# Sixteen projection blocks as quarter-sum products in a stage of their own, on one Trainium2 core

## The chip, the core and the metric

The kernel runs on one core of one Trainium2 chip. The metric is the device time of one execution in microseconds (us), the median of several runs. The core has five engines that run their own instruction streams: TensorE (PE) multiplies matrices and transposes, VectorE (DVE) and ScalarE (ACT) do elementwise work and bring results out of PSUM, GpSimd (POOL) does some elementwise work, and SyncE (SP) issues the DMA transfers. "PEld" in a profile is PE's loading of the stationary operand, which overlaps its matmuls.

## What is computed

One block of a hybrid encoder on 1024 tokens of width 1024, all in float32, with 16 learned meta tokens ahead of them:

```python
h = concat(meta_tokens, x)                       # 1040 tokens
u = rmsnorm(h, norm_mix)
a, q, k, v, r, lr, ga, gb = split(u @ w_in)      # widths 512, 256, 256, 512, 512, 16, 1024, 1024
p = (multiscale_pool(a) per group @ w_pool_mix) * pool_scale     # trailing means over 2, 4, 8, 16 tokens
y_a = p @ w_pool_out
log_a = log_sigmoid(lr @ w_gate_up + b_gate) / 16
o = gla_chunked(q / 8, k, v, log_a)              # chunks of 64 tokens, 4 heads, a state carried from chunk to chunk
o = rmsnorm(o, gla_norm) * silu(r)
y_b = o @ w_gla_out
h = h + (sigmoid(ga) * y_a + sigmoid(gb) * y_b) @ w_out
h = h + square(relu(rmsnorm(h, norm_ffn) @ w_ff1)) @ w_ff2
out = rmsnorm(h, norm_final)[16:]
```

## The kernel before

Every large product is made of three matmuls per 128 x 128 x 512 piece: each operand is split into a hi part (an fp32r copy, made by ACT) and a lo part (the rest, a subtraction on DVE), and `mm3` (L234) issues hi by hi, hi by lo and lo by hi into one PSUM bank. Activations are kept transposed: `TH` and `TL` hold the hi and lo parts of the normed input, 8 slices of 128 channels by 512 tokens, for each half of the sequence. A projection block is 128 columns of `w_in`. `project` (L245) runs it for each half of the tokens: 8 slices by 3 matmuls, so 48 matmuls of 512 columns for a block. Its weights come through the ring `W1` (class `Ring`, L57): two slots of 1024 columns, each loaded by SP into a raw buffer, copied to hi by ACT (L75) and subtracted to lo by DVE (L76; in the start stage by POOL). `drive` (L272) tops the ring up before each step.

The stages, in order:

1. `start` (L359). For each of eight tiles of 128 tokens: load, norm (`layer_norm`, L207, with `inv_sqrt`, L185), eight transposes on PE, split out of PSUM (`transposed`, L218, and L183), and the v projection of two heads for that tile (`v_tile`, L320), one tile behind. The meta tokens and the low-rank gate inputs (`lr_turn`, L344) follow.
2. Pooling (steps of L427 to L519). Four blocks of `a` (`a_block`), the trailing means and the mixing product of each (`mix_block`, L443), eight pooling gate blocks (`ga_block`, L479) and four products with `w_pool_out` (`ya_block`, L487), which multiply by the gate and store to DRAM (`ma_dram`). Gate blocks and pooling are interleaved by hand in the list at L512.
3. GLA (`gla`, L810). A chain of small matmuls, scans and state steps: `inside` (L703) makes the scores of a unit (two heads, one half of the tokens) by a level-wise decay, `across` (L735) carries the state and calls `finish` (L786). Both are generators that yield written waits in us: `inside` 4.5, 2.0 and six times LEVEL = 1.6, `across` 3.0, 2.4, and twice 1.0, 0.6, 0.6, 0.6, 4.0. There are four units. `inside` of a unit and `across` of the unit before go round by round; in each round `pour` (L813) puts filling work on PE, as much as the largest wait times PACE = 1.2, by the costs that the filling steps yield (0.64 for three matmuls). The filling work is the list `fill` (L632): k and q, the second half of v, four output gate blocks (`r_block`, L570), eight blocks of the other gate (`gb_block`, L580), and the first half of the product with `w_gla_out` (`yb_block`, L597). The order on PE is the order in which the program writes it; the other engines' order is laid out by the framework's planner, in which work written earlier goes first among what is ready.
4. Merge and output product, then the squared-ReLU MLP. The MLP's first product (`ff1`, L1080) already uses quarters: the channels and the tokens are cut in half, and for each pair of output blocks seven products of 12 matmuls (P1 to P7) of sums and differences of quarters stand for eight. The weight operands are made three products ahead (`ff1_weights`, L1012), the partial results are added up by DVE with the running sums `u2` and `u3`, and four results come out per pair (A11, A22, A12, A21).

A sigmoid (L468) is an ACT chain of Abs, Exp and Ln, one DVE operation (L474), and a last Exp.

Of the kernel before, what the change touches and what calls it, by code (L numbers as in the profile page):

```python
# [31 lines left out]
PACE, LEVEL = 1.2, 1.6  # L32
# [71 lines left out]
def kernel(  # L104
# [24 lines left out]
    banks(sc=2, mm=3, ms=3)  # L129
# [5 lines left out]
    ma_dram = dp.tile([8, 2, P, HALF], F32, name="ma_dram")  # L135
    gb_dram = dp.tile([8, 2, P, HALF], F32, name="gb_dram")
    r_dram = dp.tile([HEADS, 2, P, HALF], F32, name="r_dram")
# [103 lines left out]

    MAIN = [(0, META, HALF), (1, 0, HALF)]
# [29 lines left out]
    def drive(steps):  # L272

        for ring, aps, fn in steps:
            if fn is not start:
                for r in rings:
                    r.top_up()
# [80 lines left out]

    def start():  # L359
# [7 lines left out]
        mf = left.push("mf", [P, 6, CH], F32)  # L367
        S["vw"] = [right.push("vw0", [P, 2, KT, VP], F32R)]
# [4 lines left out]
        W1.eng = pool  # L373
        for t in range(8):
# [4 lines left out]
            if t == 3:  # L379
                W1.top_up()  # L380
            u = us[:, t % 3]
            layer_norm(xs[:, t % 4], u)
            transposed(u, t // 4, OFF[t // 4] + (t % 4) * P, ("ms", "sc"))
            if t == 0:
                nc.sync.dma_start(S["lrraw"], w_in[:, C_LR : C_LR + 16].rearrange("(k p) c -> p k c", p=P))
                load_vw(0)
                load(1)
                load(2)
                v_tile(0, 0)
            if t == 6:  # L390
                layer_norm(xm, um)
            if t > 1:
                v_tile(0, t - 1)
        transposed(um, 0, 0)
# [5 lines left out]
        W1.eng = dve  # L400
# [3 lines left out]
        nc.sync.dma_start(wgu, w_gate_up)  # L404

    one = []
    step(one, start)


    def pool_open():  # L410
# [11 lines left out]
        buffer("t1", 2)  # L422
        buffer("g", 6)
        buffer("o", 2)
        raw.lend(left.push("raw2", [P, D], F32))

# [16 lines left out]
    def mix_block(g):  # L443
        def fn():
# [9 lines left out]
            wb = (S["mw"][:, 0, g], S["mw"][:, 1, g])  # L454
            for c in halves():
                act.activation(S["ph"][:, 0, c], pp[:, c], ACT.Copy)
                dve.tensor_tensor(S["ph"][:, 1, c], pp[:, c], f32(S["ph"][:, 0, c]), ALU.subtract)
            for tag, c in zip(("ms", "sc"), halves()):
# [20 lines left out]
    def ga_block(d):  # L479
        def evac(b, half, at, n):  # L480
            t = sigmoid(b)
            g = gates[d, half] = nxt("g")
            act.activation(g, t, ACT.Exp)

        return lambda wb: project(wb, MAIN, evac)

    def ya_block(j):  # L487
        def fn(wb):
            hi, lo = (t.rearrange("p (k c) -> p k c", k=4) for t in wb)
            pm = S["pm"]  # L490
            for e in range(2):
                d, w = 2 * j + e, slice(e * P, (e + 1) * P)
                for h, c in enumerate(halves()):
                    b = bank("mm")
                    mm3(b, 4, lambda i: (hi[:, i, w], lo[:, i, w]), lambda i: (pm[:, 0, i, c], pm[:, 1, i, c]))
                    if e and h:
                        yield "free"
                    o = nxt("o")
                    dve.tensor_tensor(o, b, gates.pop((d, h)), ALU.mult)
                    nc.sync.dma_start(ma_dram[d, h], o)  # L500
                    yield 12 * 512 / 2400
# [6 lines left out]
    a_ = lambda g: step(one, a_block(g), W1, [w_cols(C_A + g * P)])  # L508
    m_ = lambda g: step(one, mix_block(g))
    g_ = lambda d: step(one, ga_block(d), W1, [w_cols(C_GA + d * P)])  # L510
# [7 lines left out]
    for f, i in ((g_, 6), (g_, 7), (y_, 3)):  # L518
        f(i)  # L519


    def gla_open():
# [4 lines left out]
        S["q"] = [left.push(f"q{h}", [P, 2, HALF], F32) for h in range(2)]  # L527
        S["v"].append(left.push("v1", [P, 2 * NC, P], F32))
# [25 lines left out]
    def q_block(p):  # L554
        def evac(b, half, at, n):
            act.activation(S["q"][half][:, p, :], b, ACT.Copy, scale=CH ** -0.5)

        return lambda wb: project(wb, MAIN, evac)

# [9 lines left out]

    def r_block(h):  # L570
        def evac(b, half, at, n):
            t = sigmoid(b)
            o = nxt("o")
            act.activation(t, t, ACT.Exp)
            dve.scalar_tensor_tensor(o, b, gnorm[:, h : h + 1], t, ALU.mult, ALU.mult)
            nc.sync.dma_start(r_dram[h, half], o)

        return lambda wb: project(wb, MAIN, evac)

# [52 lines left out]
    for p in range(2):  # L632
        step(fill, k_block(p), W1, [w_cols(C_K + p * P)])
        told(("k", p))
        step(fill, q_block(p), W1, [w_cols(C_Q + p * P)])
        told(("q", p))
        if p == 0:
            step(fill, v_second)
            step(fill, yg_open)
            told("v")  # L640
    for h in range(4):
        step(fill, r_block(h), W1, [w_cols(C_R + h * P)])
        told(("r", h))
    for d in range(8):
# [26 lines left out]
    def meta_state(p):  # L671
# [12 lines left out]
        yield 1.0  # L684
        b = bank("ms")
# [17 lines left out]
    def inside(p, half):  # L703
# [7 lines left out]
        while ("q", p) not in done:  # L711
            yield 1.0
# [22 lines left out]
    def across(p, half):  # L735
# [29 lines left out]
        ends = []  # L765
# [20 lines left out]
    def finish(p, half, g, o):  # L786
        while ("r", 2 * p + 1) not in done:
# [22 lines left out]
    def gla():  # L810
        filler = drive(fill)

        def pour(us):  # L813
            while us > 0:
# [3 lines left out]
                us -= cost  # L818

        while ("k", 0) not in done:  # L820
            pour(1e-3)
        units = [(0, 0), (1, 0), (0, 1), (1, 1)]
        old, side = [], [meta_state(0)]
        for n, u in enumerate(units + [None]):
# [9 lines left out]
            if n == 0:  # L834
                while ("k", 1) not in done:
                    pour(1e-3)
# [37 lines left out]
    def wo1_open():  # L874
# [4 lines left out]
        raw.lend(right.push("rawx0", [P, D], F32))  # L879
# [25 lines left out]

    def quad(a):
# [405 lines left out]
```

## Time and profile before

| | |
|---|---|
| median of 3 runs | 1293.3 us (1293.14 to 1293.83) |
| the profiled execution's own time | 1293.83 us |
| its span in the profile | 1292.0 us |
| busy: PE, DVE, ACT, POOL | 1258.3, 816.0, 600.6, 81.4 us |
| start stage, until the first pooling matmul | 0 to 60.4 us |
| pooling stage | 60.4 to 255.9 us |
| GLA stage with all its filling work | 255.9 to about 552.8 us |
| merge, output product, MLP | to the end |

The span runs from the first to the last instruction in the trace. The stage ends were read from the timeline on PE: the first matmul of a pooling block, the first log-decay matmul of GLA (L653), and the end of the filling work. A "window" view gives for a stretch of time the busy time of each engine with the count of instructions in brackets. A group of instructions shows its line, its engine, output and inputs, shapes, a count, the busy time in all and the mean in ns, and then the time that the engine stood idle just before them with what ended most of it.

### The profile page before, as it was taken

What the parts mean: (1) busy time and instruction counts of PE and PEld (TensorE: products, weight loads), DVE (VectorE), ACT (ScalarE), POOL (GpSimd) and SP (SyncE); (2) the same over time, 40 slices, a digit from 0 to 9 for tenths busy, and PEclk for the clock granted to TensorE, in tenths of its full rate; (3) what the DMA queues carried; (4) which work ended last, traced back from release to release, by engine and by line L of the source; (5) the groups of instructions that cost most, each with busy time, mean ns of one, the idle gap of its engine ahead of it and who ended that gap; (6) DMA issues with size and microseconds to landing.
All of it is one profiled execution on the core that took longest, in us unless ns stands there. A gap on an engine that the chain in (4) does not pass through costs nothing.

```text
span 1292.0 us, 17890 instructions
## 1 busy us (share of the span) xinstructions
PE 1258.3 (97%) x6703; PEld 1042.4 (81%) x6703; DVE 816.0 (63%) x1367; ACT 600.6 (46%) x1089; POOL 81.4 (6%) x62
## 2 busy tenths in 40 slices
PE   5999999999999999999999999999999999999997
PEld 5888888888788888878878888888887788888776
DVE  6636222263758675763788667677665777887686
ACT  6334334333456645431565455445453444444544
POOL 1000001020203120430000000000000000000000
PEclk9899999999999999999999999999999999999999
DMA  7211223210132323882225444444459873333522
GB/s 233 49 33 49 82 77 104 65 33 18 34 99 75 98 75 113 268 303 65 82 82 187 140 161 147 149 153 152 157 194 360 281 248 113 93 97 90 163 92 88
DMA packets 139191, 164.91 MB, mean 128 GB/s; under 512 B 10432, under 2 KB 84944, under 8 KB 139104
## 3 DMA queue, kind: packets, MB, share of 16 engines
q1 hardware_dynamic: 139104, 163.76, 39.2%
q8 instruction: 53, 0.87, 0.3%
q14 instruction: 34, 0.28, 0.1%
HBM read 115.50 MB, written 48.23 MB: 127 GB/s over the span
## 4 chain that ended last, share of the span: by engine, by line
PE 88%; DVE 5%; DMA 4%; ACT 1%; issue 1%; SPq 0%; DVEq 0%; ACTq 0%
PE b_mm L238 14%; PE b_mm L240 13%; PE b_mm L239 13%; PE b_o L239 7%; PE b_o L240 7%; PE b_o L238 7%; PE b_y L240 3%; PE b_y L238 3%; PE b_y L239 3%; PE b_sc L700 2%; PE b_z L239 2%; PE b_z L240 2%; PE b_z L238 2%; PE b_sc L239 2%; PE b_sc L240 2%; PE b_sc L238 2%
## 5 line engine op out<-in xcount | busy, mean ns | idle before, releaser
L238 PE MATMUL b_mm<-th,w1h 128*128 128x512 f32 (+1 forms) x496 | 189.2, 381 | 0.0
L239 PE MATMUL b_mm<-tl,w1h 128*128 128x512 f32 (+1 forms) x496 | 184.5, 372 | 0.0
L240 PE MATMUL b_mm<-th,w1l 128*128 128x512 f32 (+1 forms) x496 | 184.1, 371 | 0.0
L238 PEld LDWEIGHTS b_mm<-th,w1h 128*128 128x128 f32 x496 | 93.2, 188 | 19.8 <-issue 3.2
L240 PEld LDWEIGHTS b_mm<-th,w1l 128*128 128x128 f32 x496 | 93.3, 188 | 16.9
L239 PEld LDWEIGHTS b_mm<-tl,w1h 128*128 128x128 f32 x496 | 93.3, 188 | 14.6
L76 DVE TENSOR_TENSOR w1l<-raw,w1h 128x1024 fp32r<-128x1024 f32 x38 | 47.9, 1260 | 87.1 <-ACT w1h L75 86.6
L75 ACT ACTIVATE w1h<-raw 128x1024 fp32r<-128x1024 f32 x40 | 42.3, 1057 | 89.2 <-PE b_mm L239 88.1
L238 PE MATMUL b_o<-w1h 128*128 128x512 f32 x192 | 75.2, 392 | 2.7 <-DVE h L1135 1.7
L239 PE MATMUL b_o<-w1l,w1h 128*128 128x512 f32 x192 | 75.2, 391 | 1.3 <-DVE w1l L989 1.3
L240 PE MATMUL b_o<-w1h,w1l 128*128 128x512 f32 x192 | 74.9, 390 | 0.1
L988 ACT ACTIVATE w1h<-raw 128x512 fp32r<-128x512 f32 x88 | 54.6, 623 | 43.4 <-PE b_sc L239 14.1
L989 DVE TENSOR_TENSOR w1l<-raw,w1h 128x512 fp32r<-128x512 f32 x88 | 60.2, 684 | 11.5 <-ACT w1h L988 11.5
L474 DVE SCALAR_TENSOR_TENSOR t<-b_mm,t 128x512 f32<-128x512 f32 x40 | 27.5, 688 | 53.4 <-ACT t L473 53.3
L1183 DVE TENSOR_TENSOR bt<-w,w 128x512 f32<-128x512 f32 x80 | 54.7, 684 | 1.1 <-DMA w<-in_w_ff_dram 1.1
L988 ACT ACTIVATE w1h<-bt 128x512 fp32r<-128x512 f32 x45 | 28.4, 630 | 57.4 <-issue 33.6
L239 PE MATMUL b_o<-fxl,fxh 128*128 128x512 f32 x128 | 50.3, 393 | 0.6 <-DVE small L199 0.6
L238 PE MATMUL b_sc<-th,w1h 128*128 128x512 f32 x128 | 50.1, 391 | 0.7 <-ACT u2p L1107 0.7
L238 PE MATMUL b_mm<-wo,th 128*128 128x512 f32 x128 | 50.7, 396 | 0.0
L239 PE MATMUL b_z<-tl,w1h 128*128 128x512 f32 x128 | 49.9, 390 | 0.4 <-DVE tl L931 0.4
L239 PE MATMUL b_mm<-wo,th 128*128 128x512 f32 x128 | 50.2, 392 | 0.0
L240 PE MATMUL b_mm<-wo,tl 128*128 128x512 f32 x128 | 50.2, 392 | 0.0
(299 smaller groups left out, 3168.9 us busy)
## 6 DMA issues: line engine op xcount, KB each, us to landing
hf_dram<-h SPq DMA_DIRECT2D x112, 256.0 KB, 2.1
raw<-hf_dram SPq DMA_DIRECT2D x112, 256.0 KB, 2.7
raw<-in_w_in_dram SPq DMA_DIRECT2D x32, 512.0 KB, 4.2
w<-in_w_ff_dram SPq DMA_DIRECT2D x64, 256.0 KB, 4.8
rawx<-in_w_ff_dram SPq DMA_DIRECT2D x16, 512.0 KB, 4.1
raw<-in_w_ff_dram SPq DMA_DIRECT2D x16, 512.0 KB, 4.0
xs<-in_x_dram SPq DMA_DIRECT2D x8, 512.0 KB, 5.8
ma_dram<-o SPq DMA_DIRECT2D x16, 256.0 KB, 2.0
```

Of the source, the lines that this page charges most:

```text
L75: self.nc.scalar.activation(hi, raw, ACT.Copy)
L76: self.eng.tensor_tensor(lo, raw, hi.bitcast(F32), ALU.subtract)
L238: pe.matmul(ps, ah, bh, start=first and i == 0, stop=False, skip_group_check=more)
L239: pe.matmul(ps, ah, bl, start=False, stop=False, skip_group_check=more)
L240: pe.matmul(ps, al, bh, start=False, stop=last and i == n - 1, skip_group_check=more)
L474: dve.scalar_tensor_tensor(t, b, 0.0, t, ALU.min, ALU.subtract)
L700: pe.matmul(b[r, c], kk[r, s], qq[r, s], start=True, stop=True, tile_position=(e * CH, e * CH))
L988: act.activation(hi, a, ACT.Copy)
L989: dve.tensor_tensor(lo, a, f32(hi), ALU.subtract)
L1183: dve.tensor_tensor(bt, w, S["w2"][q[3:]][:, i], ALU.add if q[2] == "+" else ALU.subtract)
```

## The change

The scheme of the MLP's first product is taken out into a class, `Quarters`, and used a second time. The eight ga blocks, two q blocks, four r blocks and the first two gb blocks, in that order, form eight pairs, and each pair is made by seven products of 12 matmuls. They are made in a new stage, `gate_stage`, between the start stage and pooling.

- In `start`, `turned` replaces `transposed`: it also builds the four quarter sums of the activations (`ut`), by two more ACT copies for each of the first four tiles, and by one ACT copy and four DVE subtractions for each of the last four. W1 isn't loaded in the start stage any more, so POOL's splits are gone from there. Four products (P1 and P2 of the first two pairs) are issued on PE among the last four tiles.
- `gate_stage` splits the four sums into hi and lo, then runs the other 52 products. Results go through the sigmoid and out to DRAM: ga to `ga_dram` (new), q to `q_dram` (new), r and gb where they went before.
- Pooling has no gate blocks left. Its order is turned round (group 3 first), the means (`mean_block`) and the mixing product (`mix_block`) are separate steps, the first `ya_block` takes the last mixing product into its middle, and gates are loaded from `ga_dram` four ahead.
- In GLA, q is loaded from `q_dram`; `fill` holds k, v, six gb blocks and the product with `w_gla_out`. PACE is 0.91, and `pour` carries over what it poured too much (`owed`). Waits for q and r are replaced by waits for v.
- The PSUM banks of the start stage are two `mm` and four `ms` instead of three and three, of the new stage two `sc`, four `y` and two `z`.

```diff
-PACE, LEVEL = 1.2, 1.6
+PACE, LEVEL = 0.91, 1.6
...
-    banks(sc=2, mm=3, ms=3)
+    banks(sc=2, mm=2, ms=4)
...
+    class Quarters:
...
+        def run(self):
+
+            xb, zb, late = {}, {}, []
+            for p, i, (ah, al) in self.todo():
+                bh, bl = self.x[p]
...
+                mm3(b, 4, lambda k: (ah[:, k], al[:, k]), lambda k: (bh[:, k], bl[:, k]), first=not more, more=more)
+                u2 = S["u2p"][:, i % 2]
+                if p == "P1":
+                    act.activation(u2, b, ACT.Copy)
+                elif p == "P2":
+                    late.append(i)
+                yield
+                while self.room and late:
+                    n = late.pop(0)
+                    self.result(n, A11, xb.pop(n), None)
+                if p == "P6":
+                    dve.tensor_tensor(u2, b, u2, ALU.add)
+                elif p == "P7":
+                    u3 = S["u3p"][:, i % 2]
+                    dve.tensor_tensor(u3, b, u2, ALU.add)
+                    self.result(i, A22, zb[i], u3)
...
+    def turned(u, t):
...
+            if half == 0:
+                act.activation(r[j], b, ACT.Copy)
+            elif j == 0:
+                act.activation(r[2], b, ACT.Copy)
+                dve.tensor_tensor(r[0], b, r[0], ALU.subtract)
+            else:
+                dve.tensor_tensor(r[3], b, r[0], ALU.subtract)
+                dve.tensor_tensor(r[2], b, r[2], ALU.subtract)
+                dve.tensor_tensor(r[1], r[1], r[3], ALU.subtract)
...
-                W1.top_up()
...
+            if t > 3:
+                next(run)
...
+    def gate_result(i, w, b, u):
+        (kind, n, _), half = BLOCKS[2 * i + (w in (A12, A22))], int(w in (A21, A22))
+        if u is not None:
+            c = nxt("c")
+            dve.tensor_tensor(c, b, u, ALU.add)
+            b = c
+        o = nxt("o")
...
+        t = sigmoid(b)
+        if kind == "r":
+            act.activation(t, t, ACT.Exp)
+            dve.scalar_tensor_tensor(o, b, gnorm[:, n : n + 1], t, ALU.mult, ALU.mult)
+            nc.sync.dma_start(r_dram[n, half], o)
+        else:
+            act.activation(o, t, ACT.Exp)
+            nc.sync.dma_start((ga_dram if kind == "ga" else gb_dram)[n, half], o)
+
+    def gate_stage():
...
+        for p, j in (("P5", 0), ("P6", 3), ("P7", 2), ("P4", 1)):
...
+            q.x[p] = h, l = [left.push(f"ut{j}{k}", [P, 4, HALF], F32R) for k in "hl"]
+            for k in range(0, 4, 2):
+                a = S["ut"][j][:, k : k + 2]
+                act.activation(h[:, k : k + 2], a, ACT.Copy)
+                dve.tensor_tensor(l[:, k : k + 2], a, f32(h[:, k : k + 2]), ALU.subtract)
...
+        for _ in S["gate_run"]:
+            pass
...
     for f, i in (
-        (a_, 0), (a_, 1), (m_, 0), (a_, 2), (m_, 1), (a_, 3), (m_, 2), (g_, 0), (m_, 3), (g_, 1),
-        (y_, 0), (g_, 2), (g_, 3), (y_, 1), (g_, 4), (g_, 5), (y_, 2),
+        (a_, 3), (p_, 3), (a_, 2), (m_, 3), (p_, 2), (a_, 1), (m_, 2), (p_, 1), (a_, 0), (m_, 1), (p_, 0),
+        (y_, 0), (y_, 1), (y_, 2),
     ):
...
-    for d in range(8):
+    step(fill, v_second)
+    step(fill, yg_open)
+    told("v")
+    for d in range(2, 8):
         step(fill, gb_block(d), W1, [w_cols(C_GB + d * P)])
...
+        owed = [0.0]
+
         def pour(us):
-            while us > 0:
+            owed[0] += us
+            while owed[0] > 0:
                 cost = next(filler, None)
                 if cost is None:
                     return
-                us -= cost
+                owed[0] -= cost
```

More of the change, by code (lines that the diff above doesn't have):

```diff
@@ L425, in pool_open @@
         raw.lend(left.push("raw2", [P, D], F32))
+        for _ in range(4):
+            gate_load()
     step(one, pool_open)
@@ L477, with gate_load @@
     gates = {}
[L479 to L485, printed above, removed]
+    def gate_load():
+        n = len(gates)
+        if n < 16:
+            g = gates[n // 2, n % 2] = nxt("g")
+            nc.sync.dma_start(g, ga_dram[n // 2, n % 2])
     def ya_block(j):
@@ L684, in meta_state @@
         yield 1.0
+        while p and "v" not in done:
+            yield 1.0
         b = bank("ms")
```

390 lines of the change are left out of this document (214 added, 176 removed).

## The prediction

> **What bounds the kernel now.** First the page's busy shares, the slices and the chain.
>
> ```profile
> span 1292.0 us, 17890 instructions
> PE 1258.3 (97%) x6703; PEld 1042.4 (81%) x6703; DVE 816.0 (63%) x1367; ACT 600.6 (46%) x1089; POOL 81.4 (6%) x62
> ...
> PE   5999999999999999999999999999999999999997
> ...
> PE 88%; DVE 5%; DMA 4%; ACT 1%; issue 1%; SPq 0%; DVEq 0%; ACTq 0%
> ```
>
> PE is busy for 97% and carries 88% of the chain; of its 33.7 us of idle half (60.4 - 43.28, below) lies in the start stage. So time comes off where PE has fewer matmuls, and is lost where something else becomes late. I price by stage, from the windows:
>
> ```profile
> 0.00:60.40 60.40, 43.28 (x299) 40.55 (x300) 39.99 (x89) 32.33 (x78) 7.45 (x10) 0.94 0.52 151
> 10.60:60.40 49.80, 41.42 (x292) 38.98 (x292) 37.95 (x83) 28.05 (x72) 6.51 (x4) 0.93 0.46 135
> ...
> 255.90:552.80 296.90, 295.12 (x2264) 246.63 (x2263) 187.71 (x344) 149.79 (x288) 55.48 (x38) 1.00 0.29 91
> ...
> 180.00:240.00 60.00, 60.00 (x262) 48.85 (x261) 16.03 (x20) 26.84 (x39) 4.82 (x2) 1.00 0.30 84
> ...
> 700.00:950.00 250.00, 250.00 (x1100) 206.08 (x1099) 174.63 (x274) 126.85 (x211) 0.00 (x0) 1.00 0.46 151
> ```
>
> The columns after the window are its length and the busy time of PE, PEld, DVE, ACT and POOL, then clock, DMA share and GB/s. The first rows are the start stage, the third is the GLA stage. Projections (180 to 240) and the first MLP product (700 to 950) keep PE full: 60/262 = 0.2290 us and 250/1100 = 0.2273 us per matmul of 512 columns. The second window already runs the quarter scheme that the change spreads, with DVE 70% and ACT 51% busy, and PE loses nothing.
>
> **Matmuls.** Sixteen blocks leave the pooling and GLA stages: 16 x 48 = 768 matmuls, 768 x 0.2290 = 175.9 us. Eight pairs of seven products of 12 come: 672 x 0.2273 = 152.7 us, of which 48 (10.9 us) lie in the start stage and 624 (141.8 us) in the new one. Alone this is -23.2 us. With one price for both it is 96 x 0.2273 = -21.8.
>
> **Start stage.** It ends at 60.4 now. DVE is its narrow place, and POOL makes it narrower:
>
> ```profile
> 26.16 2.35 DVE L195 SCALAR_TENSOR_TENSOR small<-small 128x1 f32<-128x1 f32 x1
> ...
> 38.44 2.39 DVE L214 SCALAR_TENSOR_TENSOR us<-xs,small,gB 128x1024 f32<-128x1024 f32 x1
> ...
> L195 DVE SCALAR_TENSOR_TENSOR small<-small 128x1 f32<-128x1 f32 x8 | 3.9, 482 | 1.0 <-ACT small L193 0.5
> L200 DVE TENSOR_TENSOR small<-small 128x1 f32<-128x1 f32 x8 | 2.8, 351 | 0.1
> L214 DVE SCALAR_TENSOR_TENSOR us<-xs,small,gB 128x1024 f32<-128x1024 f32 x8 | 11.6, 1445 | 0.9 <-DMA gB<-in_norm_mix_dram 0.8
> L76 POOL TENSOR_TENSOR w1l<-raw,w1h 128x1024 fp32r<-128x1024 f32 x2 | 4.8, 2394 | 19.0 <-ACT w1h L75 19.0
> L183 DVE TENSOR_TENSOR tl<-b_ms,th 128x512 fp32r<-128x512 f32 x8 | 5.5, 688 | 0.2
> ```
>
> A one-column operation takes 2.35 us while POOL splits W1 (L76). The change takes those POOL splits and that of mw out of this stage; with undisturbed prices (estimated at 0.22, 0.16 and 1.28 us from the shorter rows of the same lines) DVE gets 2.1 + 1.5 + 1.4 = 5.0 us back. It pays: the last four token tiles have four more subtractions of 512 columns each (16 x 0.688 = 11.0), and the eight weight operands made there take eight lo parts and four sums (12 x 0.684 = 8.2, the price of L989 below): 19.2 us. From 10.6 on DVE then has 37.95 - 5.0 + 19.2 = 52.2 us; some 3.7 of it (operands of P6 and P7, last copies) isn't needed before P5. 10.6 + 48.5 + 2.5 of waits for PE's first tiles + 2.4 for the first half of the split quarter sum gives 64 for the first product P5. This assumes no other idling; ACT and DVE alternate at each tile, and I take 68. Bounds: 64 and 75 (DVE at three quarters). ACT (28.05, and 22 copies of 0.62 more) is not the bound; PE fills its idle slots with the 48 matmuls. Against now: **+7.6**.
>
> **Entry of the new stage.** Four quarter sums of 2048 columns are split: per sum two ACT copies and two DVE subtractions of 1024 columns, for P5, P6, P7, P4 in turn:
>
> ```profile
> L76 DVE TENSOR_TENSOR w1l<-raw,w1h 128x1024 fp32r<-128x1024 f32 x38 | 47.9, 1260 | 87.1 <-ACT w1h L75 86.6
> L75 ACT ACTIVATE w1h<-raw 128x1024 fp32r<-128x1024 f32 x40 | 42.3, 1057 | 89.2 <-PE b_mm L239 88.1
> ...
> L988 ACT ACTIVATE w1h<-raw 128x512 fp32r<-128x512 f32 x88 | 54.6, 623 | 43.4 <-PE b_sc L239 14.1
> L989 DVE TENSOR_TENSOR w1l<-raw,w1h 128x512 fp32r<-128x512 f32 x88 | 60.2, 684 | 11.5 <-ACT w1h L988 11.5
> L474 DVE SCALAR_TENSOR_TENSOR t<-b_mm,t 128x512 f32<-128x512 f32 x40 | 27.5, 688 | 53.4 <-ACT t L473 53.3
> ```
>
> Each sum costs DVE 2.5 us; a weight operand with its sum 1.4. A product lasts 12 x 0.2273 = 2.73. The two P5 give 5.5 us of cover, but P7 and P4 need 2.5 + 1.4 + 0.7 of DVE per 2.73 of PE, some 2 short each. With the lead of the two P5 I take **+3** (0 to 8).
>
> **The stage itself.** Per pair PE needs 84 x 0.2273 = 19.1 us. DVE: 4 sums, 7 lo parts, 2 running sums, 3 last sums, 4 sigmoid subtractions = 20 x 0.686 = 13.7, for r pairs four more, 16.5. ACT: 7 hi parts, one copy and 16 functions:
>
> ```profile
> 161.08 0.60 ACT L471 ACTIVATE t<-b_mm 128x512 f32<-128x512 f32 x1 [1.54 <-PE b_mm L240]
> 161.71 0.63 ACT L472 ACTIVATE t<-t 128x512 f32<-128x512 f32 x1
> 162.37 0.63 ACT L473 ACTIVATE t<-t 128x512 f32<-128x512 f32 x1
> 163.04 0.69 DVE L474 SCALAR_TENSOR_TENSOR t<-b_mm,t 128x512 f32<-128x512 f32 x1 [4.17 <-ACT t L473]
> 163.76 0.63 ACT L483 ACTIVATE g<-t 128x512 f32<-128x512 f32 x1 [0.76 <-DVE t L474]
> ```
>
> that is 24 x 0.62 = 14.9. Both fit under 19.1, and operands are made three products (8 us) ahead. Stores go out on SP's queue at 1 MB per pair, the MLP stage stores 2.25. I cost the stage at PE's pace: **141.8**, upper bound below.
>
> **Back into pooling.** The first pooling weights use W1's slot 0, which the last product (number 56, slot 56 mod 4 = 0) still reads. So its hi copy (1.06 on ACT) starts when PE stops, and the lo part follows (1.26); ACT is also busy with the last results. **+3** (1.2 to 6). The gate loads (256 KB per 2.73 us) run four ahead. The pooling means now lie behind the next block's matmuls; the widest has five operations of 1024 columns and two of 512, 5 x 1.26 + 2 x 0.69 = 7.7 us of DVE (priced like L76 and L989), against a block of 24 x 1040 / 512 x 0.229 = 11.2 of PE. The last mix stands before the product: of its two evacuations of 0.62 + 0.69, the second in the shade of the first, **+1** (0 to 2).
>
> Does a gap of 3 us also cost clock?
>
> ```profile
> 35.06 0.60 PE L240 MATMUL b_mm<-vw,tl 128*128 128x272 f32 x1 [3.06 <-DVE tl L183]
> ...
> 32.00:35.00 3.00, 0.00 (x0) 0.00 (x0) 2.93 (x4) 1.39 (x4) 1.20 (x2) 0.71 0.35 52
> 35.00:40.20 5.20, 5.14 (x23) 5.14 (x24) 4.93 (x13) 3.04 (x11) 1.27 (x1) 0.51 0.25 74
> ```
>
> Here 3.06 us without a matmul was followed by 5.2 us at a granted clock of 0.51, a loss of 2.6. The bounds of 6 and 8 above hold one such loss each; my values hold none, since the gaps that I expect are of 1 to 2 us, broken by matmuls. The Trainium skill, "TensorE: Matmul & The Clock Gate", section "Part 1: The HAM clock gate", has the clock fall only after an idle window of about 3.4 us. By that no gap here costs clock and the sum stays; by the row, one gap at the pooling entry would add 2.6. The trace differs from a plain reading of the page, as its gap was shorter.
>
> **GLA.** Its chain (scores, scans, states) lies between projection matmuls that are poured in by costs. q, r and two gb blocks go, 384 of the 768 matmuls, and PACE falls from 1.2 to 0.91. One unit now:
>
> ```profile
> 393.55:445.81 52.26, 52.26 (x441) 43.14 (x443) 37.49 (x69) 31.45 (x60) 11.02 (x8) 1.00 0.29 85
> ...
> L238 PE MATMUL b_mm<-th,w1h 128*128 128x512 f32 x51 | 21.2, 416 | 0.0
> ...
> L474 DVE SCALAR_TENSOR_TENSOR t<-b_mm,t 128x512 f32<-128x512 f32 x7 | 4.8, 683 | 2.1 <-ACT t L473 2.1
> L76 DVE TENSOR_TENSOR w1l<-raw,w1h 128x1024 fp32r<-128x1024 f32 x3 | 3.7, 1224 | 3.4 <-ACT w1h L75 3.4
> L575 DVE SCALAR_TENSOR_TENSOR o<-b_mm,small,t 128x512 f32<-128x512 f32 x1 | 0.7, 743 | 0.0
> ```
>
> 153 filling matmuls, 35.0 us, so PE's own GLA work is 17.2. The written waits of a round, largest of the live generators, sum to 24.7 per unit; x 0.91 / 0.64 x 3 = 105 matmuls (debts are now carried over, where rounds were rounded up before), 24.1 us. A unit shrinks to 41.3. DVE: 37.49 - 9.2 of fill = 28.3, plus 5.7 for 2.2 gb blocks, is 34.0, or 82%. It fits on average, not in the score levels:
>
> ```profile
> 402.15 0.72 DVE L731 COPY_PREDICATED scc<-mask,b_sc 128x512 f32<-128x512 uint8 x1
> ...
> 403.36 0.68 DVE L722 TENSOR_TENSOR Q<-q,E 128x512 f32<-128x512 f32 x1
> 403.96 0.34 DVE L776 SCALAR_TENSOR_TENSOR S<-S,small,b_ms 128x128 f32<-128x128 f32 x1
> 404.58 1.31 DVE L668 TENSOR_TENSOR suf<-suf,pre 128x256 f32<-128x256 f32 x1 [0.29 <-ACT E L718]
> 405.99 0.43 DVE L669 TENSOR_TENSOR pre<-pre 128x256 f32<-128x256 f32 x1
> ...
> 403.05 1.08 PE b_sc L700 x32
> ```
>
> A level takes DVE 3.5 us. PE gets 1.08 of scores, 0.2 of states and 1.6 x 0.91 / 0.64 x 3 x 0.229 = 1.6 of fill: 2.9. Six levels lack 3.6 us; about 1.6 is absorbed since a level is made one ahead. 2 us in each of three units, and 2 at the first and last one: **+8** (-2, should the waits that PE has there now go, to 20).
>
> **Sum.** -175.9 + 7.6 + 3 + 141.8 + 3 + 1 + 8 = -11.5. The profiled execution took 1293.8 us (span 1292.0 and 1.8 around it), 0.5 above the median of 1293.3: 1282.3 there, **1282** on the median.
>
> **Rivals.**
> *GLA's chain takes the freed time (slower).* If DVE's 3.5 us per level and its queue also hold each state step and finish, a unit takes 47 instead of 41.3: 3 x 5.7 more, and in all +25 instead of +8: 1299. It ends slower from a loss of 19.5, a unit of 45. For it: 82% DVE and POOL slowing L668 from 0.43 to 1.31. Against: before, PE waited only 296.9 - 295.1 = 1.8 us in the whole stage, and r's work on ACT and DVE leaves.
> *The hand-overs bound the new stage.* L474's row shows 53.4/40 = 1.33 us of DVE idle per sigmoid. If nothing can fill this, a ga pair needs 13.7 + 5.3 = 19.0 of DVE and an r pair 21.8, 2.7 over PE, twice; and the 10 us of entry splits have no slack to be made good: +15, so 1297. Against: DVE now idles there since it has nothing else, and the MLP stage, equally chained, loses nothing.
> The Trainium skill, in the same page's section "Architectural detail: the array is 16× 32×32, not 1× 128×128", calls ACT and DVE strictly first-in first-out, which speaks for this rival; no row here shows an overtaking either way.
> *All covers hold.* P5 at 64, entry 1, pooling 1.5, GLA 1: 1282 - 4 - 2 - 1.5 - 7 = 1267.
> That the change doesn't drop its 96 matmuls is hardly possible; PE's instruction count would show it.
>
> **How the numbers follow.** Forecast, with its own range of 1272 to 1290: 0.60; all covers hold: 0.14; GLA 0.14; hand-overs 0.08; both in half (within 2.6 us of now): 0.04. About 0.2% (2.6 us) can be told from no change. Faster 0.76, same 0.05, slower 0.19 (both slow rivals nearly whole). Range 1268 to 1297: it leaves out the far end of the fast case and the worse half of the slow ones.
>
> **What would show it.** PE x6607; P5's first matmul near 68 with 48 product matmuls before it; PE full in the new stage at 0.227 us each; a gap below 3 us at the first pooling matmul; PE idle in GLA, put down to DVE lines of the scan, near 10 us in all. Wrong if PE idles on DVE or ACT inside the new stage, or if GLA's units stay above 45.

## The result, and the profile after

The changed kernel takes **1299.55 us** (median of 4 runs, 1299.17 to 1300.59), the kernel before beside it 1293.22 (4 runs): ratio 1.0054, 95% interval 1.0037 to 1.0071. It is slower by 0.5%, 2.6 us above the upper end of the range. The profiled execution took 1300.59, its span 6.8 us more than before's.

The page of the changed kernel: span, busy shares, granted clock and chain.

```profile
span 1298.8 us, 18047 instructions
PE 1244.5 (96%) x6607; PEld 1027.5 (79%) x6607; DVE 897.5 (69%) x1505; ACT 632.1 (49%) x1157; POOL 75.7 (6%) x60
...
PEclk9899999999999989999999999999999999999999
...
PE 78%; DVE 10%; DMA 5%; ACT 3%; issue 2%; SPq 1%; POOL 0%; DVEq 0%; ACTq 0%
```

The 96 matmuls are gone (6703 to 6607) and PE is busy for 13.8 us less, but its idle time rose from 33.7 to 54.3 us, by 20.6. DVE's part of the chain doubled, and the clock dips in two places: in the second slice, and in the fifteenth, 455 to 487 us in. To see where, I cut both spans at the same events: first matmul after the start stage (P5 in the new kernel), first log-decay matmul of GLA, last transpose of GLA's outputs, first transpose of the MLP's input, end. Windows of the changed kernel (columns as in the prediction):

```profile
0.00:76.60 76.60, 54.39 (x345) 48.78 (x345) 54.57 (x119) 46.15 (x103) 1.55 (x7) 0.96 0.37 109
76.60:332.40 255.80, 251.57 (x1204) 209.62 (x1204) 156.38 (x217) 129.54 (x219) 9.21 (x9) 1.00 0.41 126
332.40:532.00 199.60, 188.75 (x1782) 158.07 (x1782) 148.32 (x295) 102.27 (x215) 43.94 (x31) 0.98 0.22 68
532.00:626.90 94.90, 92.57 (x397) 74.93 (x396) 48.70 (x61) 26.61 (x38) 20.99 (x13) 0.98 0.55 188
626.90:1298.80 671.90, 657.21 (x2885) 536.14 (x2883) 489.48 (x816) 327.54 (x584) 0.00 (x0) 0.99 0.46 154
```

and of the kernel before, from GLA on:

```profile
256.10:526.30 270.20, 268.42 (x2149) 225.10 (x2149) 166.15 (x319) 137.72 (x272) 41.57 (x29) 1.00 0.24 71
526.30:621.60 95.30, 94.89 (x414) 77.17 (x413) 51.57 (x66) 28.48 (x41) 24.49 (x15) 1.00 0.60 208
621.60:1292.00 670.40, 656.00 (x2885) 535.01 (x2883) 488.87 (x816) 327.61 (x584) 0.00 (x0) 1.00 0.47 154
```

Read against the forecast, stage by stage (the second row's forecast is 195.7 - 87.9 + 141.8 + 3 + 3 + 1, the third's 365.5 - 87.9 + 8, where 87.9 is 384 x 0.2290):

| stretch | before | forecast | after | miss |
|---|---|---|---|---|
| start stage, to P5 | 60.4 | 68 | 76.6 | +8.6 |
| new stage and pooling | 195.7 | 256.6 | 255.8 | -0.8 |
| GLA and merge | 365.5 | 285.6 | 294.5 | +8.9 |
| MLP | 670.4 | 670.4 | 671.9 | +1.5 |

The misses sum to 18.2, and the span grew by 6.8 where -11.5 was forecast, 18.3 away. The new stage, the largest term, came as forecast; two smaller terms were each some 9 us off.

**The start stage.** DVE and then PE around the last token tile, timeline of the changed kernel:

```profile
54.45 0.68 DVE L310 TENSOR_TENSOR fs<-fs,rawx 128x512 f32<-128x512 f32 x1
55.16 0.29 DVE L466 COPY v<-b_mm 64x128 f32<-64x128 f32 x1
55.48 0.16 DVE L202 TENSOR_TENSOR small<-small 128x1 f32<-128x1 f32 x1
55.56 0.68 DVE L310 TENSOR_TENSOR fs<-fs,rawx 128x512 f32<-128x512 f32 x1
56.16 1.28 DVE L216 SCALAR_TENSOR_TENSOR us<-xs,small,gB 128x1024 f32<-128x1024 f32 x1
...
57.58 1.30 PE L502 MATMUL b_ms<-ident,us 128*128 128x128 f32 x5 [3.14 <-DVE us L216]
```

DVE works without a break, but on the sums of weight quarters (L310), which nobody needs before P5, while PE stands 3.14 us for the last tile's norm (L216); just ahead of these rows stand the activations' quarter sums of the tile before. PE had waited longer still for another tile's norm, at 34 us:

```profile
34.22 1.06 PE L502 MATMUL b_ms<-ident,us 128*128 128x128 f32 x8 [3.50 <-DVE us L216]
```

What follows the two gaps, in windows of the same kernel, and then what follows the earlier of them in the run with thicker rounds (below), whose start stage is the same code:

```profile
34.20:38.20 4.00, 3.98 (x33) 4.00 (x34) 3.94 (x12) 3.46 (x10) 0.23 (x1) 1.00 0.00 0
58.00:63.30 5.30, 5.30 (x26) 5.30 (x25) 4.50 (x8) 3.48 (x5) 0.00 (x0) 0.51 0.00 0
34.95:38.95 4.00, 4.00 (x18) 4.00 (x19) 3.46 (x11) 3.20 (x9) 0.29 (x1) 0.50 0.00 0
```

Behind the 3.14 us come 5.3 us of matmuls at a granted clock of 0.51, so 2.6 us are lost again. Behind the longer gap of 3.50 us the clock stayed at 1.00 here, but it was 0.50 in the other run, and so it was in two more without the norm edit. So the same gap costs clock in one execution and not in another; P5 comes at 76.6 here and at 78.2 to 78.9 in those three. And behind this last tile PE still has three v tiles, a product and the low-rank turn to do before P5, which it runs nearly without a break until 75.3.

**The new stage.** Its entry, its bulk and its end:

```profile
76.60:90.00 13.40, 11.55 (x48) 8.96 (x49) 12.62 (x18) 9.58 (x16) 0.00 (x0) 1.00 0.34 93
90.00:219.00 129.00, 129.00 (x566) 105.92 (x565) 89.58 (x138) 85.36 (x149) 0.00 (x0) 1.00 0.38 115
219.00:225.00 6.00, 4.02 (x20) 3.00 (x19) 5.11 (x6) 5.97 (x10) 0.00 (x0) 1.00 0.90 298
```

PE loses 1.9 us at the entry and 2.0 at the pooling weights, nothing between, at 129/566 = 0.228 us per matmul.

**GLA.** The waits of PE in GLA and merge of the changed kernel (us in total, times, longest):

```profile
PE b_ms L1023 <- DVE on L1019: 5.8, 5, 2.0
PE b_mm L242 <- DVE w1l L76: 2.3, 2, 1.9
PE b_sc L924 <- DVE Q L944: 1.7, 1, 1.7
PE b_ms L991 <- DVE kt L981: 1.2, 1, 1.2
```

The largest is the transpose of a finished output (L1023), which waits for the norm before it (L1019). In all PE idles for 10.85 + 2.33 = 13.2 us here, against 2.2 before.

### The profile page after: what moved, and what is told of

It is laid out like the page before. It is cut to its first block, busy times and chain, and to the rows that moved or that the text cites. A ratio compares the mean times of both kernels' runs of the same rounds, so it can differ in the third digit from the quotient of the medians.

```text
span 1298.8 us, 18047 instructions
## 1 busy us (share of the span) xinstructions
PE 1244.5 (96%) x6607; PEld 1027.5 (79%) x6607; DVE 897.5 (69%) x1505; ACT 632.1 (49%) x1157; POOL 75.7 (6%) x60
## 4 chain that ended last, share of the span: by engine, by line
PE 78%; DVE 10%; DMA 5%; ACT 3%; issue 2%; SPq 1%; POOL 0%; DVEq 0%; ACTq 0%
PE b_mm L240 7%; PE b_mm L241 7%; PE b_mm L242 7%; PE b_o L241 7%; PE b_o L242 7%; PE b_o L240 7%; PE b_y L242 5%; PE b_y L240 5%; PE b_y L241 5%; PE b_sc L241 3%; PE b_sc L240 3%; PE b_sc L242 3%; PE b_z L240 3%; PE b_z L241 3%; PE b_z L242 3%
## 5 line engine op out<-in xcount | busy, mean ns | idle before, releaser
L240 PE MATMUL b_mm<-th,w1h 128*128 128x512 f32 (+1 forms) x240 | 88.4, 368 | 1.2 <-ACT w1h L75 1.2
L242 PE MATMUL b_mm<-th,w1l 128*128 128x512 f32 (+1 forms) x240 | 84.6, 353 | 0.8 <-DVE w1l L76 0.8
L241 PE MATMUL b_mm<-tl,w1h 128*128 128x512 f32 (+1 forms) x240 | 84.7, 353 | 0.0
L258 ACT ACTIVATE w1h<-raw 128x512 fp32r<-128x512 f32 x96 | 59.6, 623 | 43.9 <-PE b_sc L241 14.1
L241 PE MATMUL b_sc<-tl,w1h 128*128 128x512 f32 x192 | 75.4, 393 | 0.0
L242 PE MATMUL b_sc<-th,w1l 128*128 128x512 f32 x192 | 75.1, 391 | 0.0
L240 PE MATMUL b_z<-th,w1h 128*128 128x512 f32 x160 | 62.5, 390 | 0.6 <-DVE h L1241 0.6
L242 PE MATMUL b_z<-th,w1l 128*128 128x512 f32 x160 | 62.3, 389 | 0.0
L259 DVE TENSOR_TENSOR w1l<-fs,w1h 128x512 fp32r<-128x512 f32 x72 | 49.4, 686 | 14.0 <-ACT w1h L258 13.9
L258 ACT ACTIVATE w1h<-bt 128x512 fp32r<-128x512 f32 x45 | 28.4, 630 | 57.4 <-issue 33.7
L240 PEld LDWEIGHTS b_mm<-th,w1h 128*128 128x128 f32 x240 | 45.6, 190 | 10.9 <-issue 3.2
L242 PEld LDWEIGHTS b_mm<-th,w1l 128*128 128x128 f32 x240 | 45.7, 190 | 7.2 <-DVE w1l L76 1.0
```

The source lines that it names most:

```text
L240: pe.matmul(ps, ah, bh, start=first and i == 0, stop=False, skip_group_check=more)
L241: pe.matmul(ps, ah, bl, start=False, stop=False, skip_group_check=more)
L242: pe.matmul(ps, al, bh, start=False, stop=last and i == n - 1, skip_group_check=more)
L258: act.activation(hi, a, ACT.Copy)
L259: dve.tensor_tensor(lo, a, f32(hi), ALU.subtract)
```

## Experiments

Two theories for the start stage: the norm stands too late in DVE's order (**order**), or DVE simply has too much work. Three for GLA: its chain needs a certain amount of filling work in total, and the change takes too much away (**total**, or cover); the thinner rounds (PACE 0.91, overshoot carried to the next round) leave its steps uncovered (**thin rounds**); or DVE and ACT are too loaded by the filling work itself (**load**). Each run stood beside runs of the kernel before on the same chip (medians 1291.2 to 1292.8); ratios are to those.

**One tile ahead.** The changed kernel, with the next tile's norm written ahead of a tile's transposes:

```diff
-            layer_norm(xs[:, t % 4], u)
+            if t == 0:
+                layer_norm(xs[:, 0], u)
+            if 0 < t < 7:
+                layer_norm(xs[:, (t + 1) % 4], us[:, (t + 1) % 3])
             turned(u, t)
...
                 load(2)
+                layer_norm(xs[:, 1], us[:, 1])
```

> The changed kernel with one edit: in the start stage the norm of the next token tile is written ahead of the transposes, splits and quarter sums of the present one, so that it goes first in DVE's queue. Order theory of the start stage: the new DVE work (operand splits and sums) stands ahead of the next tile's norm, which opens PE gaps of 3.5 us at 31 to 34 and of 3.1 us at 54 to 57.6 with 2.3 us of half clock behind it; these go, and the first P5 starts at 68 to 71 instead of 76.6: 1292 to 1295 us. Rival, amount theory: DVE simply has 19 us more to do in this stage and its order doesn't matter: P5 stays within 2 us of 76.6, 1297.5 us or more.

1291.17 us, ratio 0.9992 (0.9978 to 1.0007): 8.4 below the changed kernel. The start window:

```profile
0.00:71.10 71.10, 53.75 (x346) 47.27 (x346) 54.05 (x119) 45.74 (x103) 1.72 (x7) 0.98 0.40 117
```

The same DVE work (54.05 against 54.57), but P5 5.5 us earlier and the mean clock 0.98 in place of 0.96. Both long waits for the norm are gone. It is the order, not the amount. GLA's chain is as long as before the edit (199.6); of the 11.1 us between the two profiled spans the other 5.6 lie in merge and MLP (91.7 and 669.5 against 94.9 and 671.9), which vary by so much among the runs below without a change of their code.

**Thicker rounds in the changed kernel**:

```diff
-PACE, LEVEL = 0.91, 1.6
+PACE, LEVEL = 1.2, 1.6
```

> The changed kernel with PACE 1.2 instead of 0.91 and nothing else: a third more filling work per round of GLA, of which there is 115 in cost units, so that it is used up before the last unit. Thin-round theory: PE's 13 us of waits in GLA come from rounds that hold too little work, so most go: 1290 to 1293 us. Rival, total theory: GLA's chain of four units is now longer than all the work that is left to cover it, so what the first units gain the last one loses: 1298 to 1302 us, with PE waiting in the last across steps and the waits before them gone.

1300.55, ratio 1.0067 (1.0052 to 1.0082): nothing gained. Window of the chain and the largest wait:

```profile
335.20:546.60 211.40, 197.49 (x1828) 167.82 (x1828) 161.22 (x308) 109.11 (x225) 50.59 (x36) 0.97 0.27 83
```

```profile
PE b_ms L1023 <- DVE on L1019: 11.8, 3, 5.6
```

The idle time is still 13.9 us, but now in three waits, of up to 5.6 us: the earlier rounds are covered, and the filling work runs out ahead of the last outputs.

**The four ga pairs alone.** Only they go through the new stage; q, r and gb stay in GLA as before, with before's rounds:

```diff
-    BLOCKS = (
-        [("ga", d, C_GA + d * P) for d in range(8)] + [("q", p, C_Q + p * P) for p in range(2)]
-        + [("r", h, C_R + h * P) for h in range(HEADS)] + [("gb", d, C_GB + d * P) for d in range(2)]
-    )
+    BLOCKS = [("ga", d, C_GA + d * P) for d in range(8)]
```

> Only the eight ga blocks go through the new stage (4 pairs, 336 matmuls for 384); q, r and gb are filling work of GLA as before, with PACE 1.2 and without the carried debt. Cover theory: GLA goes back to 2 us of waits and its 366 us from first log-decay matmul to the first transpose of the output product; 11 us of matmuls are saved, the start stage costs 5.3 more than the products that it holds, the entries about 4: 1292 to 1294 us, better than all eight pairs by 6 though it saves half. Rival, fixed-cost theory: the loss belongs to what the stage adds (sums, DRAM round trips, entries), so half the saving with the same fixed cost is worse than eight pairs: 1303 us or more.

1295.42, ratio 1.0016 (1.0000 to 1.0033), a little above what was expected.

```profile
259.00:529.10 270.10, 268.33 (x2148) 225.04 (x2148) 166.07 (x318) 137.76 (x272) 41.18 (x29) 1.00 0.24 72
```

GLA is again what it was before (270.2): its loss goes with its filling work and its rounds, not with the rest of the change. What is left is the start stage (P5 at 78.2).

**Before, with the thin rounds.** The kernel before with PACE 0.91 and the overshoot carried:

```diff
-PACE, LEVEL = 1.2, 1.6
+PACE, LEVEL = 0.91, 1.6
...
-            while us > 0:
+            owed[0] += us
+            while owed[0] > 0:
...
-                us -= cost
+                owed[0] -= cost
```

> The kernel before, with only GLA's pouring of the change: PACE 0.91 and carried debts, all filling work still there. Thin-round theory: the rounds are as thin as in the changed kernel, so PE waits 10 us or more in them, and the work not poured runs after the chain at full PE: 1301 to 1305 us. Total theory: what counts is how much filling work there is in all; with 88 us more of it the time stays at 1293 plus 0 to 4 us.

1315.81, ratio 1.0186 (1.0171 to 1.0201): worse than either theory had it.

```profile
255.50:510.60 255.10, 235.56 (x1978) 196.75 (x1978) 161.26 (x304) 118.65 (x241) 39.10 (x28) 0.97 0.19 54
510.60:644.70 134.10, 134.10 (x585) 109.29 (x584) 66.03 (x80) 49.97 (x73) 24.09 (x16) 1.00 0.57 190
```

With all its filling work PE idles 19.5 us in the chain (8.9 at the transposes of finished outputs, 8.0 at the states of the meta tokens), while 585 matmuls are left for afterwards. So thin rounds cost by themselves, and before's 1.8 us of waiting were the work of its thick rounds, not a slack of the chain.

**Less load.** The changed kernel, whose six gb blocks in GLA leave out the sigmoid (one ACT copy in its place, so their gates are other numbers):

```diff
-            t = sigmoid(b)
...
-            act.activation(o, t, ACT.Exp)
+            act.activation(o, b, ACT.Copy)
```

> The changed kernel, whose six gb blocks in GLA leave out their sigmoid: one ACT copy of the product takes its place, so the outputs are other numbers. Of each block 1.4 us of DVE and 3.8 us of ACT go, 8 and 23 us in all, the filling matmuls stay. If the load of DVE (82% by the forecast) makes the waits of the scan in GLA, PE's idle time there (13.2 us) falls by 5 or more and the time to 1290 to 1295. If it is the length of the chain of the scan itself against too little filling work, idle time there falls by under 3 us and the time stays at 1297 to 1300.

1299.14, ratio 1.0043 (1.0024 to 1.0062).

```profile
335.00:534.70 199.70, 190.19 (x1782) 159.93 (x1782) 140.73 (x283) 82.33 (x179) 42.32 (x31) 0.97 0.22 66
```

DVE has 7.6 us less and ACT 19.9 less in this window than after, and it is as long as after's (199.6); PE idles there for 9.5 us in place of 10.9. So the load of the filling work on DVE and ACT explains some 1.3 us of it. The scan's own work on DVE was not varied.

**The order in the kernel before**, the same edit as in the first run:

> The kernel before with the next tile's norm written one tile ahead in the start stage, nothing else. If the changed kernel's gain of 8.4 by this order came from its own added sums standing ahead of the norm, little is to be had here: 1291 to 1293.5, within 2 us. If the order was wrong in the kernel before too, the 60 us start stage, which has 17 us of idle PE, shortens by 5 to 8: 1285 to 1288, and the order is no part of the change's account.

1291.70, ratio 0.9998 (0.9990 to 1.0007), and the start stage ends at 60.4 as it did. So the order pays nothing here; it pays only with the change's own sums in the queue.

**Fewer pairs, norm ahead.** Now a ladder: 4, 5, 6 and 7 of the 8 pairs in the new stage (ga; and q; and two r; and the other two r), the norm one tile ahead, before's thick rounds in GLA, and the blocks that aren't in the stage back among GLA's filling work. For six:

```diff
-        + [("r", h, C_R + h * P) for h in range(HEADS)] + [("gb", d, C_GB + d * P) for d in range(2)]
+        + [("r", h, C_R + h * P) for h in range(2)]
...
+    for h in (2, 3):
+        step(fill, r_block(h), W1, [w_cols(C_R + h * P)])
+        told(("r", h))
-    for d in range(2, 8):
+    for d in range(0, 8):
```

Four pairs:

> Four pairs (ga alone) in the stage, with the norm one tile ahead. If the two causes, order in the start stage and cover in GLA, are separate and add up, this is the four-pair kernel (1295.4) less the gain of the norm order on the changed kernel (8.4): 1287, 1285 to 1289. If the norm order only paid because the start stage had no slack in the full change, less than half of it appears here: 1291 to 1295.

1291.07, ratio 0.9982 (0.9970 to 0.9995), half of the expected gain. The stages tell why:

```profile
0.00:71.20 71.20, 53.86 (x345) 47.32 (x345) 54.05 (x119) 45.74 (x103) 1.50 (x7) 0.98 0.40 117
...
252.00:522.20 270.20, 268.40 (x2148) 225.05 (x2148) 165.87 (x318) 137.74 (x272) 41.21 (x29) 1.00 0.24 72
522.20:620.30 98.10, 95.28 (x415) 77.27 (x414) 52.00 (x66) 28.70 (x41) 23.24 (x15) 1.00 0.59 201
620.30:1291.40 671.10, 656.77 (x2885) 536.34 (x2883) 489.39 (x816) 327.49 (x584) 0.00 (x0) 0.99 0.47 154
```

The start stage gains 7.0 of 78.2, and GLA is the same; merge and MLP took 4.4 us more in this execution than in the run without the norm edit. The 12 runs spread from 1285.0 to 1293.2, so the gain is there in its stage, and part of it is lost behind it. Over these runs the time goes with the mean granted clock: 1285.0 us at 0.999, 1293.2 at 0.994. So part of what moves between executions of one kernel is clock; what moves merge and MLP by 2 to 4 us I didn't follow further.

Five pairs:

> Five pairs (ga and q) in the stage of quarter products, r and gb left as filling work between the steps of GLA with the pacing of before, and the next tile's norm written one tile ahead in the start stage. Cover theory (GLA's loss came from taking its filling work; the rest of the change saves what its matmul counts say): the four-pair kernel ran at 1295.4, the fifth pair removes 12 more matmuls (2.7 us), the norm order gave 8.4 on the changed kernel, so 1283 to 1287, GLA's idle time 2 to 5 us. Rival (any cut in GLA's filling work costs its own size, since the chain there is the bound): q's 96 matmuls less in GLA come back as idle time there, 22 us, so no gain over the four-pair kernel with the same norm order, 1287 or above, with PE idle in GLA above 8 us.

1285.90, ratio 0.9945 (0.9930 to 0.9961), as the cover theory had it.

```profile
269.20:515.80 246.60, 245.81 (x2051) 206.84 (x2050) 165.01 (x316) 134.01 (x266) 40.56 (x29) 1.00 0.24 74
515.80:613.60 97.80, 95.86 (x418) 77.71 (x416) 54.97 (x66) 28.49 (x41) 23.96 (x15) 1.00 0.61 204
```

q's 96 matmuls leave GLA without a new wait: 0.8 us idle.

Six pairs:

> As the five-pair kernel (1285.9), with the first pair of r blocks in the stage too: 96 filling matmuls less in GLA (22 us), 12 matmuls less in all. Cover as a total: with eight pairs at this pacing GLA waited 13.9 us, about 61 matmuls' worth, so cover runs out between seven and eight pairs and the sixth pair still pays its 2.7 us: 1282 to 1284.5, GLA idle under 2 us. Rival (cover runs out gradually, from the fifth pair on, since the steps of the chain are at fixed places): GLA waits 3 to 6 us and the sixth pair pays nothing: 1285 to 1289.

**1275.51**, ratio 0.9874 (0.9860 to 0.9889): the fastest here, 15.7 below the kernel before, and 6.5 better than the better theory expected.

```profile
69.00:285.60 216.60, 214.39 (x1035) 179.18 (x1036) 128.60 (x172) 102.18 (x171) 9.65 (x9) 0.99 0.42 129
285.60:520.60 235.00, 235.00 (x2004) 198.65 (x2004) 164.66 (x317) 126.69 (x254) 46.90 (x33) 1.00 0.27 82
520.60:604.10 83.50, 83.50 (x367) 68.26 (x366) 43.39 (x56) 24.51 (x35) 17.09 (x11) 1.00 0.57 197
```

From GLA's first matmul to the MLP PE never idles. The filling work ends just with the chain: 367 matmuls are left behind it, and 350 were left with thicker rounds of the full change, where it ran out. Of the 11.4 us between this span and that of five pairs, 2.9 are the pair's own (22.0 - 19.1); 3.9 more come from GLA and merge, where five pairs had idled 2.7, and 2.5 and 1.9 from the start stage and the MLP, which the edit doesn't touch. The 2.5 are clock: behind a gap of 1.60 us at 60.65 the next 4 us ran at 1.00 here, behind one of 1.61 us at 60.51 they ran at 0.50 with five pairs.

Seven pairs:

> All four r blocks in the stage as well, the eight gb blocks left in GLA. Cover as a total: 1279 to 1283, GLA idle under 4 us, the loss of the full change comes with its last pair. Rival (gradual): GLA waits 8 to 12 us and the time is 1286 to 1291, near the eight-pair kernel with the same norm order (1291.2).

1298.83, ratio 1.0056 (1.0045 to 1.0068): both theories missed it, a cliff of 23 us behind one more pair.

```profile
308.30:543.50 235.20, 221.51 (x1923) 187.73 (x1923) 166.34 (x314) 120.78 (x243) 50.33 (x36) 0.97 0.27 83
543.50:625.70 82.20, 82.11 (x351) 66.27 (x350) 33.60 (x47) 18.88 (x29) 11.53 (x8) 0.98 0.50 170
```

GLA and merge have 97 matmuls less than with six pairs (22 us), and take 317.4 in place of 318.5 us. 13.8 us are idle time. The rest is clock, about 7 us, as the timeline around the first of the three gaps shows:

```profile
506.04 0.39 PE L241 MATMUL b_mm<-yg,w1h 128*128 128x512 f32 x1
506.27 0.40 PE L242 MATMUL b_mm<-yg,w1l 128*128 128x512 f32 x1
509.30 0.94 PE L1036 MATMUL b_ms<-ident,on 128*128 128x128 f32 x4 [2.63 <-DVE on L1032]
...
511.32 0.63 PE L240 MATMUL b_mm<-yg,w1h 128*128 128x512 f32 x1
511.75 0.63 PE L241 MATMUL b_mm<-yg,w1h 128*128 128x512 f32 x1
```

Ahead of the gap a matmul starts every 0.23 us, behind it every 0.43.

**Seven pairs with carried overshoot**, the rounds of the second run (PACE 1.2):

```diff
-            while us > 0:
+            owed[0] += us
+            while owed[0] > 0:
...
-                us -= cost
+                owed[0] -= cost
```

> The seven-pair kernel, with rounds of GLA that carry their overshoot to the next round (as in the changed kernel) at the pacing number of before, 1.2: thinner rounds, the same filling work. In the seven-pair kernel the filling work ran out in the last unit: three waits of up to 5.7 us, 13.8 us idle, and slow matmuls behind them. If only the distribution was wrong there, the thinner rounds leave enough for the last unit: idle in GLA under 4 us, 1273 to 1282. If the filling work is too little in total, the idle time moves to other rounds: 10 us or more, 1290 to 1299.

1288.10, ratio 0.9956 (0.9936 to 0.9976), between the two.

```profile
311.10:527.90 216.80, 213.42 (x1908) 180.23 (x1908) 158.11 (x306) 115.56 (x236) 47.16 (x33) 1.00 0.26 80
```

The idle time of the chain falls from 13.7 to 3.4 us: for seven pairs it was mostly the distribution. Yet the time stays 12.6 above six pairs, since the stage and the pooling grow by 23.6 us (19.1 for 84 matmuls, 3.4 of idle time that six pairs don't have there) and GLA and merge shrink only by 14.2.

**Six pairs with the change's rounds**, the last diff and

```diff
-PACE, LEVEL = 1.2, 1.6
+PACE, LEVEL = 0.91, 1.6
```

> The six-pair kernel (1275.5, no idle time in GLA), with the rounds of the changed kernel: pacing 0.91, overshoot carried. If thin rounds by themselves expose the chain of the scan, whatever filling work is left over, GLA waits 10 us or more while over 40 us of filling work are left behind it, and the time is 1286 to 1298. If only the total of the filling work counts, there is enough of it here: idle under 4 us, 1274 to 1279.

1290.25, ratio 0.9983 (0.9971 to 0.9995).

```profile
283.60:482.20 198.60, 186.99 (x1783) 157.68 (x1782) 146.70 (x292) 102.10 (x216) 38.30 (x28) 0.99 0.18 52
482.20:617.10 134.90, 134.90 (x588) 109.95 (x587) 66.44 (x80) 50.25 (x74) 25.38 (x16) 1.00 0.56 188
```

The chain takes 198.6 us with 1783 matmuls and 11.6 of idle time: the same as in the changed kernel (199.6, 1782, 10.9), though 588 matmuls wait behind it. So thin rounds alone are enough for the waits of the change.

All of GLA and merge side by side. "Expected" takes 22.0 us (96 x 0.2290) off before's 365.5 for each pair that leaves GLA:

| kernel | pairs out of GLA | rounds | expected | measured | loss | idle |
|---|---|---|---|---|---|---|
| before | 0 | 1.2, rounded up | 365.5 | 365.5 | | 2.2 |
| before, thin | 0 | 0.91, carried | 365.5 | 389.2 | 23.7 | 19.5 |
| four pairs, norm | 0 | 1.2, rounded up | 365.5 | 368.3 | 2.8 | 4.6 |
| five | 1 | 1.2, rounded up | 343.5 | 344.4 | 0.9 | 2.7 |
| six | 2 | 1.2, rounded up | 321.5 | 318.5 | -3.0 | 0 |
| six, thin | 2 | 0.91, carried | 321.5 | 333.5 | 12.0 | 11.6 |
| seven | 3 | 1.2, rounded up | 299.5 | 317.4 | 17.9 | 13.8 |
| seven | 3 | 1.2, carried | 299.5 | 304.3 | 4.8 | 5.4 |
| eight, PACE 1.2 | 4 | 1.2, carried | 277.5 | 294.0 | 16.5 | 14.7 |
| the change | 4 | 0.91, carried | 277.5 | 294.5 | 17.0 | 13.2 |

Neither theory is enough alone. With plenty of filling work thin rounds lose 12 to 24 us. With the full change, thicker rounds lose as much (16.5 us), since the work runs out first. PACE alone was varied with the full change, the carrying of overshoot alone with seven pairs, and where filling work is plentiful only both together. Whether some rounds would cover all eight pairs is open.

## Why the prediction was wrong

- **What bounds the kernel: half right.** PE does bound it, and its 1.8 us of waiting in GLA were read as "the chain has slack". The thin rounds in the kernel before show what they were: 19.5 us of waits come up as soon as the same work is poured in thinner.
- **Matmuls, right.** PE x6607; the stage ran at 0.228 us per matmul (0.2273 forecast).
- **Start stage, +7.6 forecast, +16.2 measured; failed.** The sum took DVE as one queue of work and asked when it would be done, with "64" and a margin. The amount was right (DVE was busy for 54.6 us in this stage; 40.0 before and the 14.2 forecast are 54.2). The step that failed is the order, which the sum left out: the new sums stand ahead of the next tile's norm in that queue, so PE waits 3.50 and 3.14 us and then, in part, runs at half clock. With the norm moved ahead P5 is at 68.8 to 71.5 in seven runs, without it at 76.6 to 78.9 in four, so about 8 us are the order (shown). The seven fall into two groups: 68.8 to 69.0 where the clock stayed at 1.00 behind a gap of 1.60 us (six pairs, six thin, seven), and 70.9 to 71.5 where it fell to 0.50 to 0.64 over the next 4 us behind one of 1.59 to 1.61. So with the right order and the full clock the forecast of 68 holds, and the rest over it is clock.
- **Entry, stage and pooling: right.** 1.9 us idle at the entry (3 forecast), 2.0 at the first pooling weights (3 forecast), full between; the hand-overs don't bind. The reason given for the second gap, the last product's use of W1's slot 0, is borne out by the ladder: PE's idle time from P5 to GLA is 4.2 to 5.6 us with 4, 7 and 8 pairs (28, 49 and 56 products, of which the last one reads this slot), and 2.2 to 2.4 with 5 and 6 (35 and 42, the slot free two products and one product earlier). One number beside it was misread: the MLP stage stores 1.75 MB per pair (112 stores of 256 KB for 16 pairs), not 2.25; nothing turned on it.
- **GLA, +8 forecast, +16.9 measured; failed.** The step set DVE's 3.5 us per level against PE's 2.9 and priced the difference. Taking 7.6 us of DVE and 19.9 of ACT away took 1.3 us off the idle time of 10.9, so the load of the filling work was the wrong measure. The bound is the latency from one step of the chain to the next, covered only by what a round pours in; the largest waits sit at the finishing norm (5.8 us), while the score levels, where the step put most of its loss, took 1.7. The rounds' total, which the step computed (a unit of 41.3; measured 51.7 and 43.9 for the second and third), says nothing of what each wait needs. The rival for GLA named the stage and the sign, with a chance of 0.14, but with DVE's queue as the mechanism; that its 1299 meets the measured time is luck, as half of the miss lies in the start stage.
- **Clock: the term put at nothing was not nothing.** The values held no loss for gaps, since gaps of 1 to 2 us were expected. One of 3.14 us came in the start stage, with the price that the row of before had given (2.6). Shorter ones cost clock too: behind gaps of 1.87 us (at 568) and 1.91 us (at 976) the next 4 us ran at 0.57 and 0.69, and merge and MLP have mean clocks of 0.98 and 0.99 where both had 1.00 before. The Trainium skill, "TensorE: Matmul & The Clock Gate", section "Part 1: The HAM clock gate", gives about 3.4 us without work. Here 1.6 us were enough in four runs, and 3.50 us were not in the changed kernel. No run settles which gap is followed by slow matmuls.
- **The sign.** Start (+8.6) and GLA (+8.9) are each enough to bring the forecast of -11.5 near zero; both together turned it.

## What to carry to other kernels

Work that fills another stage's waits has a second value beside its own time: before it is made cheaper elsewhere, count how much of it the waits need, round by round, and stop where it runs out; here six pairs gave -1.3% and seven, with the same rounds, +0.6%. A bound engine's low waiting time shows that its cover holds, not that the chain beneath has slack; thinning the cover in the old kernel shows which it is. On an engine that works in order, put what the busiest engine waits for ahead of what is merely due later, above all where a gap on the busiest engine can also halve its rate for some us behind it.

## What the runs showed of the hardware

- A gap without matmuls was followed by slow ones in some executions and not in others, at the same length. Behind 3.50 to 3.52 us in the start stage the next 4 us ran at a granted clock of 1.00 in the changed kernel and of 0.50 in three other runs. Behind 1.59 to 1.61 us they ran at 1.00 in three runs and at 0.50 to 0.64 in four. Behind 2.63 us they ran at 1.00 with thicker rounds, and in the seven-pair kernel a matmul started every 0.43 us in place of 0.23.
- Where slow matmuls followed, they could take back the gain: in the seven-pair kernel 13.8 us of idle time came with some 7 us of slower matmuls, so that 1.1 of the 22 us by which its GLA and merge have fewer matmuls than with six pairs were left.
- Taking a fifth of the ACT work (102.3 to 82.3 us) out of a stage that was 51% ACT-busy did not shorten it at all.
